# Four token blocks of a mixture layer: transposed indices made ahead, block 3's weights queued behind fixed dots, block 1 alone over 88 value tiles, 48 rows of block 4 in the ring

## The chip, the cores and the metric

One core of a Trainium2 chip runs the whole kernel in one launch. The metric is the device time of an execution in microseconds (us), lower is better. The engines are PE (TensorE), DVE (VectorE), ACT (ScalarE), POOL (GpSimd) and SP (SyncE, which only issues transfers here); each works off its own instructions in order, and 16 DMA engines serve all of them.

## The reference, cut to what matters

The layer is attention, an mLSTM and a merge, and then the channel mixer below, over 512 prompt tokens and 8 sample tokens (D = 1024, 8 heads, top 16, 16384 experts). The change touches only the last part.

```
q   = xb @ wq;  s = q . subkeys            # two halves of 128 keys each
s1, i1 = top_k(s[half 0], 16);  s2, i2 = top_k(s[half 1], 16)
top_s, eidx = the best 16 of s1 + s2;  g = softmax(top_s)
act = gelu(xb . u[eidx])                   # 128 rows of u for each token
out = sum over 128 of (g * act) * v[eidx]  # 128 rows of v for each token
y   = x + out
```

## The kernel before, in words

A scheduler puts the instructions of each engine into a fixed order, by the order in which the source emits them (earlier is more urgent) and by when its own simulation has each one ready. On the chip an engine then waits at each instruction until what it needs is there; nothing overtakes. `tc.issue_after(ins)` puts the instructions of its block that run on the engine of `ins` behind `ins` in that engine's order.

The prompt is four blocks of 128 tokens. Blocks 1 and 2 come from the first half of the prompt (`halves[0]`), blocks 3 and 4 from the second (`halves[1]`).

**u.** For each block `gather` (L1126) issues 128 indirect transfers on POOL (L1115), each with one row of 4 KB for each of 128 tokens (512 KB), into `ring`, a pool of 6 buffers. DVE multiplies each with the block's `xn2` and sums (the dot, L1122) into a column of `S`. `xn2` is one buffer for all blocks, loaded by SP at L1110. After 128 dots `gelu_w` (L1131) makes the final `S` out of them.

**v, blocks 1 to 3.** These multiply weights over all experts with all of v. `w_block` (L1162) makes a block's weights: it transposes `i1`, `i2` and `S` on PE (L1150, copied out of PSUM by ACT at L151), and for each of 32 groups of 4 tokens makes one-hot matrices (DVE at L1173 and L1178, POOL at L1176, ACT at L148 and L1183), multiplies them on PE (L1190) and copies the product into the weights `WT` by ACT (L151). The weights of a block are two halves of 64 tiles, 32 KB a partition each. `v_part` (L1194) then streams v in 128 tiles of 512 KB through 5 buffers (SP, L1196) and, for each block in `use`, does two products of 128x512 (L1200; four instructions). `v_done` adds x and stores.

**v, block 4.** It has no weights: `v_rows_acc` (L1210) gathers 128 rows of v for each token like u (L1214), and DVE adds each, times its `S`, to `acc` (L1216). 

The order at the end, as emitted from L1325 on:

- weights of block 1; `late()` (the top-k of block 4); u of block 3, in which the first step of the sample tokens' top-k is emitted at k = 48
- tiles 0 to 63 for block 1 alone (`JH` = 64)
- weights of block 2, whose PE part stands behind tile 27 (`JW`)
- tiles 64 to 127 for blocks 1 and 2
- u of block 4, with u of the 8 sample tokens between
- weights of block 3, into the buffers of block 1's weights (`wr`, two halves), so not before block 1 is done
- tiles 0 to 63 for blocks 2 and 3, then tiles 64 to 127 for block 3 alone. Beside the latter the rows of block 4: they use `slab`, 16 slots of 4 KB in the two buffers of block 2's weights, and for the first 32 rows every other one uses the ring
- the sample tokens' v rows (L1253, into the ring, multiplied on PE at L1256) and their result (`x1s`, loaded by SP into a buffer of the value tiles)

The lines around the change:

```
useA1 = (v_acc(1), wA1, JH, JH - 1)
for j in range(JH, P):
    v_part(j, [useA0, useA1])
v_done(0, useA0[0])
gather(1, 1, ...)
wB0 = w_new(wr, wr)
w_block(selB[0], wB0, wr, pst_d, 2)
for j in range(JH):
    v_part(j, [useA1] + ([useB0] if j >= JC else []))
```

Of the kernel before, what the change touches and what calls it, by code (L numbers as in the profile page):

```python
# [5 lines left out]
F32 = mybir.dt.float32  # L6
F32R = mybir.dt.float32r
BF16 = mybir.dt.bfloat16
# [7 lines left out]
P = 128  # L16
# [37 lines left out]
EARLY = True  # L54
JH, JC, JW = 64, 0, 27
SLOPES = [2.0 ** (-(h + 1)) for h in range(8)]


def step_kernel(
# [1048 lines left out]
    def gather_dot(d, tok, off, steps, every):  # L1108
        xn2 = keep.tile([P, D], F32, tag="xn2", name="xn2", bufs=1)
        nc.sync.dma_start(xn2, scr_xn2[tok:tok + P])  # L1110
        for k in range(P):
            if steps and k % every == 0:
                next(steps, None)
            gt = ring.tile([P, D], F32, tag="g", name="urow")
            d["rows"] = nc.gpsimd.indirect_dma_start(  # L1115
                out=gt, out_offset=None, in_=u_rows,
                in_offset=bass.IndirectOffsetOnAxis(ap=d["e"][:, k:k + 1], axis=0))
            if off and k % off == off - 1:
                nc.gpsimd.tensor_mul(gt, gt, xn2)
                nc.scalar.activation(gt, gt, AF.Copy, accum_out=d["S"][:, k:k + 1])  # L1120
            else:
                d["dot"] = nc.vector.scalar_tensor_tensor(gt, gt, 1.0, xn2, op0=ALU.mult, op1=ALU.mult,  # L1122
                                                          accum_out=d["S"][:, k:k + 1])

    def gather(hf, i, y=None, steps=None, every=1):
# [19 lines left out]

    def w_prep(sel, pool, pst_):
        out = []
        for key in ("i1", "i2", "S"):
            p = pst_()
            nc.tensor.transpose(p[:, 0:P], sel[key], ident)  # L1150
            t = pool.tile([P, P], BF16 if key == "i1" else F32, tag=f"T_{key}", name=f"T_{key}", bufs=1)
            copy(t, p[:, 0:P])
            out.append(t)
            if key == "i2":
                t = pool.tile([P, P], F32, tag="T_n2", name="T_n2", bufs=1)
                copy(t, p[:, 0:P], scale=-1.0)
                out.append(t)
        return out

    iota4 = []  # L1160

    def w_block(sel, wT, pool, pst_, no):  # L1162
        ONA, PM = ONAS[no], PMS[no]
        if not iota4:
            t = pool.tile([P, P, TG], BF16, name="iota4")
            nc.vector.tensor_copy(t, iota.unsqueeze(2).to_broadcast([P, P, TG]))
            iota4.append(t)
        i1T, i2T, ni2T, sT = w_prep(sel, pool, pst_)
        for g in range(P // TG):
# [10 lines left out]
            for t in range(ONA):  # L1180
                act(b[:, t, :], iota, AF.Abs, bias=ni2T[:, t0 + t:t0 + t + 1])
            if ONA:
# [27 lines left out]
    def v_rows_acc(d, tok, acc, slot):  # L1210
        nc.sync.dma_start(acc, scr_x1[tok:tok + P])
        for k in range(P):
            gt = slot()
            nc.gpsimd.indirect_dma_start(out=gt, out_offset=None, in_=v_rows,  # L1214
                                         in_offset=bass.IndirectOffsetOnAxis(ap=d["e"][:, k:k + 1], axis=0))
            nc.vector.scalar_tensor_tensor(acc, gt, d["S"][:, k:k + 1], acc, op0=ALU.mult, op1=ALU.add)  # L1216
            yield
        nc.gpsimd.dma_start(y_prompt[0, tok:tok + P], acc)

    def sample_peer(py):  # L1220
# [30 lines left out]
        for b in range(NS):  # L1251
# [6 lines left out]
            yield  # L1258
        x1s = dv[0].tile([NS, D], F32, tag="v", name="x1s", bufs=VB)
        nc.sync.dma_start(x1s, scr_x1s)  # L1260
        for q in range(2):
# [5 lines left out]
    for hf in range(2):  # L1267
# [50 lines left out]
        if hf == 1:  # L1318
            alt = [0]

            def pst_w():
                alt[0] ^= 1
                return pst("ao"[alt[0]])

            wA0 = w_new(wr, wr)  # L1325
            w_block(halves[0][0][0], wA0, wr, pst_w, 0)
            late()
            py = []
            steps = sample_peer(py)
            gather(1, 0, None, (next(steps) if k == 48 else None for k in range(P)), 1)  # L1330
            useA0 = ([pst("a"), pst("o")], wA0, 0, P - 1)
            with tc.issue_after(sel[1]["score"].ins):
                mms = [v_part(j, [useA0]) for j in range(JH)]
        if hf == 0 and SV == 1:
# [24 lines left out]

    useA1 = (v_acc(1), wA1, JH, JH - 1)  # L1360
    for j in range(JH, P):
        v_part(j, [useA0, useA1])
    v_done(0, useA0[0])
    gather(1, 1, lambda: wr.tile([P, P], F32, name="ge_y", bufs=1),
           (next(steps) if k % 8 == 4 and k < 68 else None for k in range(P)))
    wB0 = w_new(wr, wr)
    w_block(selB[0], wB0, wr, pst_d, 2)
    useB0 = (v_acc(2), wB0, JC, (JC - 1) % P)
    for j in range(JH):
        v_part(j, [useA1] + ([useB0] if j >= JC else []))  # L1370
# [4 lines left out]
    def gslot():  # L1375
        k = slot_i[0]
        slot_i[0] += 1
        if k < 32:
            return ring.tile([P, D], F32, tag="g", name="vrow") if k % 2 else slab[0][:, k // 2 % 7 + 1, :]
        i = k % 15 + 1  # L1380
        return slab[i // 8][:, i % 8, :]

    run = v_rows_acc(selB[1], HALF + P, slab[0][:, 0, :], gslot)
    for j in [*range(JH, P), *range(JC)]:
        v_part(j, [useB0])
# [44 lines left out]
```

## Time and profile before

| | us |
|---|---|
| median of 3 runs | 2266.93 (2264.25 to 2271.74) |
| the profiled execution's own time | 2271.8 |
| its span (first to last instruction) | 2270.1 |

The profile is of one execution. Times in its rows count from the start of its span. A timeline row gives the start, the time taken, the engine, the line, the operation with its tiles (out<-in), how many were merged, and in brackets how long the engine sat idle before and what ended that. In the rows `ps_a` and `ps_o` are block 1's sums, `y` those of blocks 2 and 3, `ps_w` the products of `w_block` and of the sample rows, `urow` a gathered row of u, `vrow` and `vslab` gathered rows of v, `T_S`, `T_i` the transposed `S`, `i1` and `i2`.

### The profile page before, as it was taken

To read this page: it belongs to the slowest core of one execution; us is meant where nothing else is said; L and a number is where in the kernel's file an instruction comes from. 1 tells how busy PE (TensorE), PEld (TensorE's weight loads), DVE (VectorE), ACT (ScalarE), POOL (GpSimd) and SP (SyncE) were. 2 spreads that over 40 slices of the span, in tenths; PEclk is the share of its full clock that TensorE was granted. 3 is DMA by queue.
4 is the path that set the end of the run, shared out by engine and by line. 5 is a ranking of instruction groups with operands and counts; after the bars stand their busy time and mean duration, and the time that the engine had idled before them with its cause. 6 is when DMAs were issued, how large, how long until landed. Compare 5 with 4: busy or idle time off the path is not lost. (4 is left out here: it accounts for less than half of the span.)

```text
span 2270.1 us, 25459 instructions
## 1 busy us (share of the span) xinstructions
PE 1977.4 (87%) x7694; PEld 1312.6 (58%) x7694; DVE 1536.7 (68%) x3504; ACT 655.4 (29%) x1775; POOL 1307.7 (58%) x1226
## 2 busy tenths in 40 slices
PE   6999999888989999899897984989999699986817
PEld 4675777777878777787775732634445544431202
DVE  2355576787698977777886698855626856536694
ACT  3343233311344433334534315910014600000000
POOL 0487783453486645676776377554415854545573
PEclk9997999999988999999997997999999699997959
DMA  5685776889698889999988297899969899999999
GB/s 158 199 271 203 236 242 214 276 281 325 221 323 286 299 280 340 343 355 340 325 313 321 87 347 262 309 380 409 409 238 355 279 404 409 409 376 417 417 392 369
DMA packets 297803, 704.78 MB, mean 310 GB/s; under 512 B 31518, under 2 KB 157530, under 8 KB 297666
## 3 DMA queue, kind: packets, MB, share of 16 engines
q0 software_dynamic: 114224, 415.84, 49.1%
q1 hardware_dynamic: 183010, 285.74, 35.8%
q10 hardware_dynamic: 432, 1.57, 0.2%
q8 instruction: 61, 1.00, 0.2%
q14 instruction: 76, 0.62, 0.1%
HBM read 684.87 MB, written 18.18 MB: 310 GB/s over the span
## 5 line engine op out<-in xcount | busy, mean ns | idle before, releaser
L1115 POOL DMA_INDIRECT urow<-in_peer_u,k_e x512 | 602.2, 1176 | 394.9 <-DVE urow L1122 279.5
L1122 DVE SCALAR_TENSOR_TENSOR urow<-urow,xn 128x1024 f32<-128x1024 f32 x512 | 643.7, 1267 | 176.4 <-DMA urow<-in_peer_u,k_e 171.7
L1200 PE MATMUL y<-vtile,WT 128*128 128x512 f32 x1024 | 467.4, 601 | 73.6 <-DMA vtile<-in_peer_v 73.1
L291 PE MATMUL ps_mm<-x,wch 128*128 128x264 f32 (+1 forms) x1536 | 384.0, 403 | 27.5 <-DVE sig L315 20.2
L1200 PEld LDWEIGHTS y<-vtile,WT 128*128 128x128 f32 x1024 | 192.2, 192 | 337.5 <-issue 230.2
L291 PEld LDWEIGHTS ps_mm<-x,wch 128*128 128x128 f32 x1536 | 300.4, 200 | 83.9 <-DVE sig L315 23.5
L835 POOL TENSOR_TENSOR kpage<-kpage,qb 128x1024 f32<-128x1024 f32 x64 | 150.2, 2360 | 72.1 <-DMA qb<-scr_q 64.7
L291 PE MATMUL ps_mm<-hT,wch 128*128 128x256 f32 (+1 forms) x768 | 184.8, 390 | 3.9 <-DVE sig L315 3.6
L1214 POOL DMA_INDIRECT vslab<-in_peer_v,k_e x112 | 131.6, 1175 | 87.2 <-DMA vslab<-in_peer_v,k_e 37.7
L1216 DVE SCALAR_TENSOR_TENSOR vslab<-vslab,k_S 128x1024 f32<-128x1024 f32 x112 | 143.9, 1285 | 44.6 <-DMA vslab<-in_peer_v,k_e 41.9
L291 PEld LDWEIGHTS ps_mm<-hT,wch 128*128 128x128 f32 x768 | 143.1, 193 | 26.4 <-DVE sig L315 4.0
L1200 PE MATMUL ps_a<-vtile,WT 128*128 128x512 f32 x256 | 135.4, 611 | 18.4 <-DMA vtile<-in_peer_v 18.3
L296 PE MATMUL ps_mm<-wch,x 128*128 128x256 f32 (+1 forms) x640 | 150.0, 386 | 0.0
L823 POOL DMA_INDIRECT vpage<-in_cache_v,kidx x64 | 79.1, 1236 | 107.6 <-DVE vacc L901 68.1
L1200 PE MATMUL ps_o<-vtile,WT 128*128 128x512 f32 x256 | 132.3, 599 | 0.0
L296 PEld LDWEIGHTS ps_mm<-wch,x 128*128 128x128 f32 (+1 forms) x640 | 108.0, 174 | 29.5 <-issue 2.8
L901 DVE SCALAR_TENSOR_TENSOR vacc<-vpage,aS,vacc 128x128 f32<-128x128 f32 x384 | 110.6, 359 | 18.6 <-DMA vpage<-in_cache_v,kidx 18.4
L148 ACT ACTIVATE oh<-iota,T_n 128x128 f32<-128x128 f32 x352 | 113.4, 403 | 0.1
L1190 PE MATMUL ps_w<-oh,oh 128*128 128x128 f32 x512 | 81.1, 313 | 31.6 <-POOL oh L1176 23.9
L1190 PEld LDWEIGHTS ps_w<-oh,oh 128*128 128x128 f32 x512 | 74.3, 219 | 52.1 <-POOL oh L1176 33.6
L1176 POOL TENSOR_TENSOR oh<-ohe,T_S 128x128 f32<-128x128 bf16 (+1 forms) x96 | 69.7, 733 | 53.2 <-ACT T_S L151 37.3
L836 DVE TENSOR_REDUCE sK<-kpage 128x16 f32<-128x1024 f32 x64 | 77.3, 1211 | 29.1 <-POOL kpage L835 29.0
(428 smaller groups left out, 2728.1 us busy)
## 6 DMA issues: line engine op xcount, KB each, us to landing
vtile<-in_peer_v SPq DMA_DIRECT2D x256, 512.0 KB
wch<-in_w_in SPq DMA_DIRECT2D x256, 256.0 KB
wch<-in_peer_wq SPq DMA_DIRECT2D x64, 256.0 KB
wch<-in_w_branch_a SPq DMA_DIRECT2D x32, 256.0 KB
wch<-in_w_branch_b SPq DMA_DIRECT2D x32, 256.0 KB
wch<-in_w_out SPq DMA_DIRECT2D x32, 256.0 KB
urow<-in_peer_u,k_e POOLq DMA_INDIRECT x512, 7.9
qb<-scr_q SPq DMA_DIRECT2D x8, 512.0 KB
```

Source lines behind the costliest of these rows:

```text
L148: nc.scalar.activation(out, in_, func, bias=b[:n, 0:1] if b.shape[0] != n else b, scale=scale, **kw)
L291: nc.tensor.matmul(out, w[:, c0:c0 + m], xk[:, :n], start=(k == 0 and i == 0), stop=(k == KT - 1 and i == len(tt) - 1))
L296: nc.tensor.matmul(out, x[:, k, t0:t0 + m], ch[k // KP][:, k % KP, :n], start=(k == 0), stop=(k == KT - 1))
L823: nc.gpsimd.indirect_dma_start(out=t, out_offset=None, in_=rows, in_offset=bass.IndirectOffsetOnAxis(ap=kidx[:, b * 8 + pg:b * 8 + pg + 1] ...
L835: (nc.vector if KDV and pg % KDV == KDV - 1 else nc.gpsimd).tensor_mul(kt, kt, qb)
L901: nc.vector.scalar_tensor_tensor(acc[:, h, :], vt[:, h, :], wa, acc[:, h, :], op0=ALU.mult, op1=ALU.add)
L1115: d["rows"] = nc.gpsimd.indirect_dma_start(out=gt, out_offset=None, in_=u_rows, in_offset=bass.IndirectOffsetOnAxis(ap=d["e"][:, k:k + 1], ...
L1122: d["dot"] = nc.vector.scalar_tensor_tensor(gt, gt, 1.0, xn2, op0=ALU.mult, op1=ALU.mult, accum_out=d["S"][:, k:k + 1])
L1190: nc.tensor.matmul(pw[:, t, :], b[:, t, :], a[:, t, :], start=True, stop=True)
L1200: mm = nc.tensor.matmul(py[q], w, vt[:, q * 512:(q + 1) * 512], start=(j == j0), stop=(j == j1))
L1214: nc.gpsimd.indirect_dma_start(out=gt, out_offset=None, in_=v_rows, in_offset=bass.IndirectOffsetOnAxis(ap=d["e"][:, k:k + 1], axis=0))
L1216: nc.vector.scalar_tensor_tensor(acc, gt, d["S"][:, k:k + 1], acc, op0=ALU.mult, op1=ALU.add)
```

## The change

- `w_prep` keeps its transposes with the block, makes only those asked for, in two buffers instead of one, and no longer makes the negated copy `T_n2` (ACT negates the other operand instead). Block 2's three are emitted right behind block 1's weights, ahead of `late()`; block 3's `i1` and `i2` behind block 1's `v_done`; block 3's `S` inside its `w_block`.
- Block 3's `w_block` stands behind block 4's dot 24 on DVE and its gather 30 on POOL.
- Block 1 goes alone over tiles 0 to 87 (`NA` = 88), blocks 1 and 2 over 88 to 127, blocks 2 and 3 over 0 to 87, block 3 alone over 88 to 127.
- The first 48 rows of block 4 all use the ring; `acc` lies in the buffer of `xn2` and is loaded from POOL's queue; `x1s` lies in the ring and is loaded from POOL's queue.

```diff
-JH, JC, JW = 64, 0, 27
+JH, JC, JW, NA, HB = 64, 0, 27, 88, (24, 30)
@@ gather_dot
+            d.setdefault("gets", []).append(d["rows"])
...
+                d.setdefault("dots", []).append(d["dot"])
@@ w_prep
-    def w_prep(sel, pool, pst_):
-        out = []
-        for key in ("i1", "i2", "S"):
+    def w_prep(sel, pool, pst_, keys=("i1", "i2", "S")):
+        T = sel.setdefault("T", {})
+        for key in keys:
             p = pst_()
             nc.tensor.transpose(p[:, 0:P], sel[key], ident)
...
+            T[key] = pool.tile([P, P], BF16 if key == "i1" else F32, tag=f"T_{key}", name=f"T_{key}", bufs=2)
+            copy(T[key], p[:, 0:P])
@@ w_block
-        i1T, i2T, ni2T, sT = w_prep(sel, pool, pst_)
+        w_prep(sel, pool, pst_, [k for k in ("i1", "i2", "S") if k not in sel.get("T", {})])
+        i1T, i2T, sT = (sel["T"][k] for k in ("i1", "i2", "S"))
...
-                act(b[:, t, :], iota, AF.Abs, bias=ni2T[:, t0 + t:t0 + t + 1])
+                act(b[:, t, :], iota, AF.Abs, scale=-1.0, bias=i2T[:, t0 + t:t0 + t + 1])
@@ v_rows_acc
-        nc.sync.dma_start(acc, scr_x1[tok:tok + P])
+        nc.gpsimd.dma_start(acc, scr_x1[tok:tok + P])
@@ sample_peer
-        x1s = dv[0].tile([NS, D], F32, tag="v", name="x1s", bufs=VB)
-        nc.sync.dma_start(x1s, scr_x1s)
+        x1s = ring.tile([NS, D], F32, tag="g", name="x1s")
+        nc.gpsimd.dma_start(x1s, scr_x1s)
@@ the order
             w_block(halves[0][0][0], wA0, wr, pst_w, 0)
+            w_prep(halves[0][0][1], wr, pst_w)
             late()
...
-                mms = [v_part(j, [useA0]) for j in range(JH)]
+                mms = [v_part(j, [useA0]) for j in range(NA)]
...
-    useA1 = (v_acc(1), wA1, JH, JH - 1)
-    for j in range(JH, P):
+    useA1 = (v_acc(1), wA1, NA, NA - 1)
+    for j in range(NA, P):
         v_part(j, [useA0, useA1])
     v_done(0, useA0[0])
+    w_prep(selB[0], wr, pst_d, ("i1", "i2"))
...
-    w_block(selB[0], wB0, wr, pst_d, 2)
+    with tc.issue_after(selB[1]["dots"][HB[0]].ins), tc.issue_after(selB[1]["gets"][HB[1]].ins):
+        w_block(selB[0], wB0, wr, pst_d, 2)
...
-    for j in range(JH):
+    for j in range(NA):
         v_part(j, [useA1] + ([useB0] if j >= JC else []))
...
-        if k < 32:
-            return ring.tile([P, D], F32, tag="g", name="vrow") if k % 2 else slab[0][:, k // 2 % 7 + 1, :]
+        if k < 48:
+            return ring.tile([P, D], F32, tag="g", name="vrow")
...
-    run = v_rows_acc(selB[1], HALF + P, slab[0][:, 0, :], gslot)
-    for j in [*range(JH, P), *range(JC)]:
+    acc = keep.tile([P, D], F32, tag="xn2", name="acc", bufs=1)
+    run = v_rows_acc(selB[1], HALF + P, acc, gslot)
+    for j in [*range(NA, P), *range(JC)]:
         v_part(j, [useB0])
```

## Rows read from the trace of the kernel before

**Rows 1.** Windows by stage: us, five engines' busy time, clock, DMA share, GB/s

```profile
1305.00:1505.00 200.00, 152.29 (x532) 78.33 (x532) 163.16 (x495) 100.79 (x292) 134.62 (x170) 0.93 0.85 314
1505.00:1731.00 226.00, 221.02 (x525) 98.58 (x524) 114.37 (x193) 6.56 (x19) 92.33 (x93) 0.99 0.93 364
1731.00:1811.00 80.00, 54.19 (x264) 43.50 (x262) 70.47 (x127) 65.68 (x196) 62.28 (x67) 0.75 0.83 291
1811.00:2024.00 213.00, 212.34 (x493) 93.65 (x494) 110.82 (x195) 2.93 (x9) 100.49 (x99) 1.00 1.00 397
2024.00:2270.00 246.00, 143.90 (x288) 48.70 (x286) 164.64 (x131) 0.00 (x0) 140.25 (x123) 0.83 0.99 399
```

**Rows 2.** Windows of the whole end and of single stretches, same columns

```profile
1305.00:2265.00 960.00, 783.22 (x2097) 362.77 (x2096) 622.38 (x1135) 175.96 (x514) 529.98 (x550) 0.92 0.94 365
...
1367.00:1395.00 28.00, 0.40 (x3) 0.14 (x1) 23.25 (x68) 6.92 (x14) 24.66 (x28) 0.59 0.62 218
...
1655.00:1697.00 42.00, 42.00 (x112) 19.66 (x111) 5.52 (x11) 3.69 (x12) 2.74 (x5) 1.00 0.55 204
...
2024.00:2163.00 139.00, 101.65 (x204) 33.27 (x202) 89.07 (x71) 0.00 (x0) 84.46 (x72) 0.90 1.02 415
2163.00:2218.00 55.00, 1.98 (x4) 0.68 (x4) 52.94 (x43) 0.00 (x0) 41.30 (x40) 0.54 1.00 387
```

**Rows 3.** Timeline of PE, block 1 alone and then with block 2

```profile
1338.36 1.12 PE L1200 MATMUL ps_a<-vtile,WT 128*128 128x512 f32 x2 [0.56 <-DMA vtile<-in_peer_v]
...
1340.91 1.13 PE L1200 MATMUL ps_a<-vtile,WT 128*128 128x512 f32 x2 [0.57 <-DMA vtile<-in_peer_v]
...
1395.40 0.47 PE L1150 MATMUL ps_w<-ident,k_S 128*128 128x128 f32 x1 [28.00 <-ACT T_i L151]
...
1519.00 1.88 PE L1200 MATMUL y<-vtile,WT 128*128 128x512 f32 x4
...
1522.43 1.88 PE L1200 MATMUL y<-vtile,WT 128*128 128x512 f32 x4
...
1729.47 1.02 PE L1200 MATMUL ps_o<-vtile,WT 128*128 128x512 f32 x2
```

**Rows 4.** Timeline of DVE: first one-hot of block 2

```profile
1398.95 1.39 DVE L1173 TENSOR_TENSOR ohe<-iota,T_i 128x512 bf16<-128x512 bf16 x3
```

**Rows 5.** Timeline of DVE: block 3's last dot, its first one-hots, block 4's first dot

```profile
1650.20 1.23 DVE L1122 SCALAR_TENSOR_TENSOR urow<-urow,xn 128x1024 f32<-128x1024 f32 x1 [0.87 <-DMA urow<-in_peer_u,k_e]
...
1689.57 1.23 DVE L1178 TENSOR_TENSOR oh<-ohe,T_S 128x384 f32<-128x384 bf16 x2 [34.24 <-ACT T_S L151]
...
1695.46 1.21 DVE L1122 SCALAR_TENSOR_TENSOR urow<-urow,xn 128x1024 f32<-128x1024 f32 x1
```

**Rows 6.** Timeline of SP's queue: block 4's load of xn2

```profile
1679.22 0.42 SPq L1110 DMA_DIRECT2D xn<-scr_xn  x1
```

**Rows 7.** Window of urow's instructions: DVE (two records a dot), POOL, clock, DMA

```profile
1505.00:1655.00 150.00, 88.26 (x144) 67.39 (x70) 0.99 1.03 408
```

**Rows 8.** Groups by line, 1731 to 1811: busy, mean ns, idle before

```profile
L1115 POOL DMA_INDIRECT urow<-in_peer_u,k_e x31 | 37.8, 1219 | 11.0 <-issue 4.9 <-DVE urow L1122 3.9 <-DVE urow_s L1244 1.2
L151 ACT ACTIVATE WT<-ps_w 128x256 f32<-128x256 f32 x61 | 20.0, 382 | 14.3 <-PE ps_w L1190 14.1
L1183 ACT ACTIVATE oh<-oh,one 128x512 f32<-128x512 f32 x27 | 19.1, 727 | 0.1
```

**Rows 9.** Timeline of POOL: sample rows, the wait for block 2, the last store

```profile
1994.75 0.94 POOL L1253 DMA_INDIRECT vrow_s<-in_peer_v,eT  x1 [0.30 <-DVE ge_y L1137]
...
2022.52 0.94 POOL L1214 DMA_INDIRECT vslab<-in_peer_v,k_e  x1 [19.17 <-PE y L1200]
...
2260.18 0.59 POOL L1218 DMA_DIRECT2D out_y_prompt<-vslab  x1 [19.46 <-DVE vslab L1216]
```

**Rows 10.** Timeline of PE: the first product of sample rows

```profile
2023.89 1.88 PE L1256 MATMUL ps_w<-vrow_s,wz 128*8 128x512 f32 x4
```

**Rows 11.** Waits of SP's queue, 1650 to 2270

```profile
SPq L1196 <- DMA out_y_sample<-x1s: 55.8, 1, 55.8
```

More of the change, by code (lines that the diff above doesn't have):

```diff
@@ L1144, in w_new @@
         return [(pool.tile([P, JH, P], F32, tag="WT", name="WT", bufs=2), JH * i) for i, pool in enumerate(pools)]
-    def w_prep(sel, pool, pst_):
-        out = []
-        for key in ("i1", "i2", "S"):
+    def w_prep(sel, pool, pst_, keys=("i1", "i2", "S")):
+        T = sel.setdefault("T", {})
+        for key in keys:
             p = pst_()
             nc.tensor.transpose(p[:, 0:P], sel[key], ident)
[L1151 to L1158, printed above, removed]
+            T[key] = pool.tile([P, P], BF16 if key == "i1" else F32, tag=f"T_{key}", name=f"T_{key}", bufs=2)
+            copy(T[key], p[:, 0:P])
     iota4 = []
```

## The prediction

> **What bounds the kernel now.** The windows by stage come first, since every edit lies behind 1305 us. They show five stages [rows 1]: block 1 alone (200 us), blocks 1 and 2 (226), block 3's weights (80), blocks 2 and 3 (213), block 3 alone beside block 4's rows (246). The reader is to look at the DMA share and at PE together. Stage 4 is PE's (212 of 213 us), stage 2 nearly so. Stage 5 is the DMA's: share 0.99, PE 144 of 246. Stage 3 is neither's: PE 54 of 80, DMA 0.83. Over the whole end DMA moved 365 GB/s on average, where full stretches show 408 and 415 [rows 2, 7], so some 11% of 960 us, about 105 us, is DMA time left unused. Single stretches then say where: 28 us at 218 GB/s and 42 us at 204 [rows 2], beside stage 3 at 291 [rows 1].
>
> Timelines say why. At 1367 PE stands 28 us before block 2's third transpose, waiting for an ACT copy [rows 3], while DVE and POOL work off block 4's top-k (23 and 25 of 28 us) [rows 2]; ACT's copy stands in order behind its own share of that. At 1655 block 3's dots are done, but DVE's next instruction is a one-hot of block 3 that waits 34 us for `T_S`, which PE transposes only where its order has it; block 4's dots are queued behind, and the first runs at 1695.46 [rows 5]. With the ring full, gathers stop: that is the 204 GB/s.
>
> **The rule weighed.** Stretches of 139 and 150 us ran at 415 and 408 GB/s [rows 2, 7], and the sums below go by 415. The Trainium skill ("DMA: Bandwidth & Descriptors", Specifications) gives HBM about 358 GB/s per core; by that figure the end, at 365, would have no DMA time left, and the sum would come to nothing. The trace disagrees with it, by those two stretches.
>
> **The change part by part.** I compare with the profiled execution (span 2270, own time 2271.8, 4.9 us above the median of the runs, 2266.93) and carry the difference to the median.
>
> *1. 24 tiles for block 1 alone (64 to 87).* With block 2 a tile takes 3.43 us (1519.00 to 1522.43), PE's own pace; alone, beside gathers, 2.55 (1338.36 to 1340.91), where PE waits for the tile [rows 3]. So block 1 ends 24 x (3.43 - 2.55) = 21 us sooner. Block 2's 24 products move to stage 4.
>
> *2. Block 2's transposes ahead.* The 28 us [rows 3] can go wholly or stay under another name: DVE, at 23 of 28 us, makes one-hots only behind the top-k, the first at 1398.95 [rows 4], and PE reaches their products at the same place behind tile 27. Ends 0 and -28. Two groups can be ready beforehand (`OH1` = 2), each worth 2.86 us: stage 3 took 80 us for its last 28 groups (L1183 runs once a group, 27 times in the stage, the first groups having come earlier), with ACT busy for 66 of them [rows 1, 8]. I take -6, because DVE's row is the nearest. The transposes and copies themselves, and the three copies less, are under 0.5 us each and lie beside other work; should PE meet them before block 2's `S` is there, the bound is the 28 us of the same kind of wait. So block 1 ends at 1731 - 21 - 6 = 1704 (1682 to 1710).
>
> *3. The gate.* Gathers of block 3 get 2.08 us each beside stage 2 (144 records, two a dot, in 150 us [rows 7]) and 2.55 beside single tiles; 24 tiles at 2.55 are 61 us, 24 gathers instead of 29, so its last dot moves from 1651 to about 1662. DVE and POOL no longer stand in the 34 us wait. With the load of `xn2` (an estimate of 5 us: 0.524 MB at half of 415 GB/s are 2.5 us, doubled for what is queued ahead) block 4's dot 0 runs at 1667 instead of 1695. By 1704 18 of 25 dots are done; 7 more at about 1.6 us (no tiles are being loaded then; POOL's 1.22 and a gap [rows 8] is the lower bound, 2.08 the upper) put the gate at 1715, 11 us behind block 1's end. What is queued behind it: DVE's and POOL's one-hots, and on PE all but five tiles of block 2.
>
> *4. Block 3's weights.* 32 groups, none ahead on DVE; three of ACT's can be (`OHB` = 3). 29 x 2.86 = 83 us (80 to 91): done at 1798, before 1811: -13.
>
> *5. Stage 4.* five tiles, of which block 2's part was done in stage 3, at 1.72 (half of 3.43) and 83 at 3.43: 293 us, to 2091. The same working gives 211 for the 213 before [rows 1]. Gathers here: of u, 128 - 30 - 31 [rows 8] = 67, then 48 rows of v and 8 sample rows, 123 x 2.08 = 256 us, below 293, so all 48 can be in. `acc` loaded from POOL's queue waits for block 4's last dot with the v gathers behind it; about the six buffers of the ring, 6 x 2.08 = 12 us, covered by the 37 left over. Without that cover what is late goes to stage 5 at 1.26 us a row.
>
> *6. Stage 5.* 35 tiles and 80 rows are 115 x 0.524 MB / 415 GB/s = 145 us, and from the last add to the end 10 us, as after 2260.18 [rows 9]: 2246. POOL's wait of 19 us for block 2's buffers [rows 9] goes for the first 48 rows, which need none of them; it is late next at row 48, at the end of stage 4. `x1s` leaves the tiles' buffers: SP waited 56 us for its store [rows 11], but DMA then still ran at 387 GB/s [rows 2], so at most 55 x (1 - 387/415) = 4 us, not counted. SP loses two transfers; POOL gains two of about 0.6 us.
>
> Sum: -13 (weights ready), +80 (stage 4), -91 (stage 5 with its end) = -24; median 2266.9 - 24 = **2243 us**.
>
> **The rivals.**
>
> *A. More.* The gate falls no later than block 1's end, because block 3's gathers run ahead: weights start at 1704, or at 1682 if the 28 us go too. Weights done 11 to 33 us sooner: 2210 to 2232. For it: 24 dots need only 50 us. Against: in the sum they get 37. 0.20.
>
> *B. Slower: the load of `xn2` stands behind tiles in SP's queue.* Before, it was issued at 1679.22 [rows 6], 28 us after the buffer was free (last dot 1650.20 [rows 5]), as SP's order has it behind tile loads that wait for buffers. With block 1 ending sooner, that place can be behind the last of its tiles: block 4's dot 0 at about 1706, 25 dots with sample rows between at 1.6 to 2.08 us, 45 us, gate 1751, weights done 1834, end 36 us later than my sum: 2279. It decides from a dot 0 later than about 1691 (24 us after my 1667). Against it: gathers were 28 us ahead of that order, which is leeway the other way too. 0.20.
>
> *C. No change: the ring fills with sample rows.* A sample row holds a ring buffer until PE multiplies it; the first, issued at 1994.75 [rows 9], was multiplied at 2023.89, after stage 4 [rows 10]. One is emitted for every four rows, so after 24 rows all six buffers could be held until stage 4 ends. Then 24 rows more fall to stage 5: +30 us, 2273. Against: at 1994 stage 4 had only 30 us left. 0.13.
>
> *D. No change: DMA is at its limit already.* If the mean of 365 GB/s [rows 2] were all that DMA sustains over such a mix, the same bytes would take the same time in any order: 2267. Against it: two long stretches at 408 and more [rows 2, 7]. 0.04. This is what the page's figure above would mean.
>
> **How the numbers follow.** My sum has 0.43. Faster by over 0.3% (7 us, about what a measurement of this kernel can tell from no change): the sum and A, 0.63, and a little of B where the 28 us go as well (its 2279 falls to 2257): 0.65. Within 0.3%: C and D less a third, 0.13. Slower: B's rest and C's longer end, 0.22. The sum's own bounds (the gate by 2.08 instead of 1.6, weights 80 to 91, stall 0 to -28, 4 us of `x1s`) reach from 2226 to 2256; the range goes on to A's middle and to B: 2214 to 2281.
>
> **What would show it.** Right: PE's 28 us before L1150 gone, with a shorter wait for DVE's or POOL's one-hots near 1370; no 34 us wait for `T_S`; block 4's dot 0 near 1667; weights of block 3 ready near 1798; stage 4 of some 293 us with PE full and gathers of v in it from about 1945; stage 5 of some 150 us. Wrong: a dot 0 behind 1700 (B); fewer than 30 rows of v gathered before block 2 ends (C); PE idle inside stage 4; a weights stage longer than 91 us, or a stall of PE ahead of 1305, where block 2's transposes now stand.

## The result and the profile after

The changed kernel takes 2294.84 us (median of 7 runs, 2288.67 to 2305.27), the kernel before beside it 2271.74 (7 runs, 2260.3 to 2281.0). The ratio is 1.0119, 95% interval 1.0089 to 1.0150: **slower by about 27 us** by the ratio (23 by the two medians), where 24 us faster was forecast, and above the range (2214 to 2281). The profiled execution is the longest of its seven (own time 2305.27, span 2303.6), so its stages, not its total, are what to compare.

The first view is the windows by stage of the changed kernel (window, length, busy time of PE, PE's weight loads, DVE, ACT and POOL with records, PE's clock, DMA share, GB/s). The boundaries: start of the double tiles, end of block 1, first products of block 3's weights, their end, end of block 2.

```profile
1310.00:1575.00 265.00, 200.00 (x615) 96.21 (x615) 193.26 (x536) 93.86 (x272) 159.68 (x195) 0.91 0.90 336
1575.00:1713.00 138.00, 137.43 (x322) 60.66 (x321) 68.93 (x117) 1.88 (x5) 53.34 (x56) 1.00 0.98 387
1713.00:1752.00 39.00, 12.58 (x25) 4.65 (x24) 28.03 (x49) 0.00 (x0) 25.28 (x24) 0.71 0.94 343
1752.00:1848.00 96.00, 60.96 (x263) 52.55 (x264) 90.28 (x162) 71.65 (x212) 83.66 (x84) 0.62 0.84 284
1848.00:2154.00 306.00, 305.34 (x706) 129.34 (x705) 140.37 (x185) 1.91 (x5) 126.05 (x123) 1.00 0.93 358
2154.00:2304.00 150.00, 80.47 (x165) 27.91 (x163) 99.66 (x80) 0.00 (x0) 82.30 (x70) 0.85 0.96 388
```

Beside [rows 1] the reader sees five stages become six: there is a new one of 39 us in which PE works 12.6. Since both kernels move the same bytes (length times rate, summed, is 351 MB in each), the DMA rate is a ledger of what each stage costs. Against 400 GB/s, about the rate of the last two stages before, a stage loses its length times (1 - rate/400):

| stage | lost before, us | lost after, us |
|---|---|---|
| block 1, alone and with block 2 | 43 + 20 | 42 + 4 |
| gate and block 3's weights | 22 | 6 + 28 |
| blocks 2 and 3 (stage 4) | 2 | 32 |
| the last stage | 1 | 4 |

That is 88 us before, 116 after: 17 us are won ahead of block 1's end, 12 are lost at the gate and the weights, 30 in stage 4. The ledger is accounting: it says in which stage time is lost, not why.

The second view is the timeline of DVE from block 3's last dot to the gate.

```profile
1667.04 1.23 DVE L1123 SCALAR_TENSOR_TENSOR urow<-urow,xn 128x1024 f32<-128x1024 f32 x1 [0.51 <-DMA urow<-in_peer_u,k_e]
...
1685.22 1.23 DVE L1123 SCALAR_TENSOR_TENSOR urow<-urow,xn 128x1024 f32<-128x1024 f32 x1 [13.06 <-DMA xn<-scr_xn]
...
1712.07 0.69 DVE L1204 TENSOR_TENSOR x1r<-x1r,ps_a 128x512 f32<-128x512 f32 x1 [6.38 <-PE ps_a L1197]
...
1736.85 1.23 DVE L1241 SCALAR_TENSOR_TENSOR urow_s<-urow_s,xb 128x1024 f32<-128x1024 f32 x1 [3.38 <-DMA xb<-scr_xn2s]
...
1745.44 1.14 DVE L1170 TENSOR_TENSOR ohe<-iota,T_i 128x512 bf16<-128x512 bf16 x3
```

The 34 us before `T_S` [rows 5] are gone, and block 4's dot 0 is 10 us earlier. But DVE then stands in order: 13 us for `xn2`, 6 for block 1's last product (its addition comes after only nine dots), and the first one-hot of block 3, which ran at 1689 before, runs at 1745. On PE the two waits are:

```profile
1404.70 2.08 PE L1187 MATMUL ps_w<-oh,oh 128*128 128x128 f32 x8 [30.45 <-POOL oh L1173]
...
1751.78 0.58 PE L1187 MATMUL ps_w<-oh,oh 128*128 128x128 f32 x1 [22.24 <-POOL oh L1173]
```

The first answers to the 28.00 us of [rows 3]: the wait has another name and the same length. The second is new. In block 3's weights the groups by line (1752 to 1846; busy and mean ns, then idle before) show two engines nearly full:

```profile
L1123 DVE SCALAR_TENSOR_TENSOR urow<-urow,xn 128x1024 f32<-128x1024 f32 x43 | 53.9, 1261 | 2.1 <-DMA urow<-in_peer_u,k_e 1.9
L1115 POOL DMA_INDIRECT urow<-in_peer_u,k_e x44 | 52.5, 1194 | 10.5 <-issue 6.8 <-DVE urow L1123 1.8 <-DVE urow_s L1241 0.9
```

43 dots and 44 gathers stand among the one-hots, where 31 gathers did [rows 8]: 13 gathers more at 1.19 us are 15 us more of POOL's time, and the stage is 16 us longer. DVE, with their dots, is busy 90 of 96 us. That the extra gathers and dots make the length is read from these rows and not tested by itself; the last section shows a second difference in them, POOL's one-hots lasting longer beside dots. In stage 4, windows of 20 us around its end (2154) and the timeline of POOL show the DMA going idle:

```profile
2100.00:2120.00 20.00, 20.00 (x48) 8.90 (x47) 13.92 (x11) 0.00 (x0) 6.48 (x5) 1.00 0.84 331
2120.00:2140.00 20.00, 20.00 (x48) 8.86 (x47) 1.49 (x2) 0.00 (x0) 2.97 (x3) 1.00 0.69 252
2140.00:2160.00 20.00, 20.00 (x48) 8.81 (x47) 1.37 (x2) 0.00 (x0) 4.30 (x5) 1.00 0.58 198
2160.00:2180.00 20.00, 14.96 (x31) 4.93 (x29) 10.11 (x8) 0.00 (x0) 10.34 (x11) 1.00 1.03 420
```

```profile
2154.48 0.94 POOL L1211 DMA_INDIRECT vslab<-in_peer_v,k_e  x1 [30.90 <-PE y L1197]
```

By 2124 the 48 rows are gathered, and eleven more into the first of block 2's two buffers; for the second POOL waits 31 us, where it waited 19 [rows 9]. Some 20 of the 32 us lost in stage 4 are lost here. Most of the rest is lost from 1970 to 2072, at 321 to 376 GB/s, where POOL waits 36 us in all for products of sample rows, which hold buffers of the ring, and 18 for DVE's additions. The sample products run in this stage, eight of this form (timeline of PE):

```profile
2007.88 1.88 PE L1253 MATMUL ps_w<-vrow_s,wz 128*8 128x512 f32 x4
```

### The profile page after: what moved, and what is told of

Read it like the earlier page. It is cut to its first block, busy times and chain, and to the rows that moved or that the text cites. A ratio compares the mean times of both kernels' runs of the same rounds, so it can differ in the third digit from the quotient of the medians.

```text
span 2303.6 us, 25448 instructions
## 1 busy us (share of the span) xinstructions
PE 1991.1 (86%) x7694; PEld 1321.9 (57%) x7694; DVE 1537.8 (67%) x3504; ACT 653.3 (28%) x1772; POOL 1308.9 (57%) x1228
## 5 line engine op out<-in xcount | busy, mean ns | idle before, releaser
L1197 PE MATMUL y<-vtile,WT 128*128 128x512 f32 x1024 | 460.8, 599 | 26.2 <-DMA vtile<-in_peer_v 25.8
L1187 PE MATMUL ps_w<-oh,oh 128*128 128x128 f32 x512 | 92.6, 343 | 89.8 <-POOL oh L1173 82.3
L1211 POOL DMA_INDIRECT vslab<-in_peer_v,k_e x80 | 93.6, 1170 | 96.3 <-DMA vslab<-in_peer_v,k_e 32.2
L1187 PEld LDWEIGHTS ps_w<-oh,oh 128*128 128x128 f32 x512 | 84.1, 247 | 109.0 <-POOL oh L1173 97.0
L1213 DVE SCALAR_TENSOR_TENSOR acc<-vslab,k_S,acc 128x1024 f32<-128x1024 f32 x80 | 102.8, 1286 | 44.8 <-DMA vslab<-in_peer_v,k_e 43.0
L148 ACT ACTIVATE oh<-iota,T_i 128x128 f32<-128x128 f32 x352 | 114.0, 406 | 0.1
L1213 DVE SCALAR_TENSOR_TENSOR acc<-vrow,k_S,acc 128x1024 f32<-128x1024 f32 x48 | 61.6, 1284 | 69.5 <-DMA vrow<-in_peer_v,k_e 61.9
L1197 PEld LDWEIGHTS ps_a<-vtile,WT 128*128 128x128 f32 x256 | 44.9, 196 | 98.7 <-DMA vtile<-in_peer_v 68.6
```

What stands on the lines that cost most here:

```text
L148: nc.scalar.activation(out, in_, func, bias=b[:n, 0:1] if b.shape[0] != n else b, scale=scale, **kw)
L1187: nc.tensor.matmul(pw[:, t, :], b[:, t, :], a[:, t, :], start=True, stop=True)
L1197: mm = nc.tensor.matmul(py[q], w, vt[:, q * 512:(q + 1) * 512], start=(j == j0), stop=(j == j1))
```

## The experiments

Block 1's first product lies between 1290 and 1313 us in these profiles, with the work upstream the same, so stages are counted from that product. Ratios are against the kernel before, run on the same chip.

| run | ratio, 95% interval | first product to end, us |
|---|---|---|
| kernel before | 1 | 964 |
| the change | 1.0119 (1.0089 to 1.0150) | 993 |
| e1 no gate | 1.0094 (1.0060 to 1.0128) | 984 |
| e2 64 tiles | 1.0084 (1.0055 to 1.0114) | 981 |
| e3 ring undone | 1.0256 (1.0221 to 1.0291) | 1019 |
| e4 `xn2` from ACT | 1.0116 (1.0086 to 1.0145) | 995 |
| f1 96 rows in the ring | 1.0113 (1.0087 to 1.0138) | 993 |
| f2 sample rows last | 1.0132 (1.0104 to 1.0160) | 991 |
| f3 f1, f2 and no gate | 1.0133 (1.0103 to 1.0163) | 991 |
| f4 `JW` = 44 | 1.0022 (0.9995 to 1.0049) | 967 |
| i1 gate sooner | 1.0064 (1.0036 to 1.0092) | 977 |
| i2 `JW` = 44, no gate | 0.9986 (0.9959 to 1.0013) | 961 |
| g1 64 tiles, no gate | 1.0081 (1.0052 to 1.0110) | 979 |
| g2 the same, `JW` = 36 | 0.9997 (0.9970 to 1.0024) | 958 |
| before and 88 tiles (g3) | 1.0005 (0.9978 to 1.0033) | 968 |
| before and ring (h1) | 1.0038 (1.0009 to 1.0067) | 978 |
| before and transposes (h2) | 1.0033 (1.0000 to 1.0066) | 973 |
| before and gate (h4) | 1.0114 (1.0075 to 1.0153) | 994 |
| before and `JW` = 36 (g0) | 0.9964 (0.9934 to 0.9993) | 955 |
| before, 88 tiles, `JW` = 44 (h3) | 0.9901 (0.9866 to 0.9935) | 947 |

### One thing taken from the change

**e1: no gate.**

```
-    with tc.issue_after(selB[1]["dots"][HB[0]].ins), tc.issue_after(selB[1]["gets"][HB[1]].ins):
-        w_block(selB[0], wB0, wr, pst_d, 2)
+    w_block(selB[0], wB0, wr, pst_d, 2)
```

> The changed kernel without the gate: block 3's weights wait for nothing but their operands, the rest of the change stays. Theory (the gate costs the time): block 3's first one-hot runs within 5 us of block 1's end near 1712 instead of at 1745, its weights are done near 1815 instead of 1846, and the time falls by 20 to 30 us, to a ratio of 0.998 to 1.003 against the kernel before. Rival (the gate only moves dots from behind the weights to ahead of them, and the same gathers have to be made later): weights done earlier as well, but block 4's dots end later and its rows of v move to the last stage, so the time falls by less than 10 us, ratio 1.008 to 1.013.

Measured: the weights' last product ends 489 us behind the first product, against 534, and the time falls by only 0.25%, with intervals that overlap. The windows of stage 4 and the last stage say where 45 us went:

```profile
1782.00:2085.60 303.60, 303.60 (x701) 130.88 (x700) 143.06 (x224) 2.81 (x8) 133.39 (x131) 0.99 0.96 376
2085.60:2275.80 190.20, 85.71 (x176) 30.02 (x174) 136.54 (x109) 0.00 (x0) 103.35 (x97) 0.77 0.96 378
```

The last stage is 40 us longer: gathers of u that the gate had ahead of the weights now lie in stage 4, and rows of v fall to the end. The rival is right: a sooner start of the weights is paid back in gathers.

**e2: 64 tiles** (`NA` 88 to 64).

> The changed kernel with 64 tiles for block 1 alone instead of 88. Theory (PE stands idle ahead of the gate, so what the 24 tiles save ahead of it is lost, and their products come back in stage 4 at 1.7 us each): block 1 ends near 1731, the gate falls at about the same 1745, stage 4 has 24 double tiles fewer, and the time falls by 10 to 25 us, ratio 1.001 to 1.008. Rival (the 24 tiles save their 21 us as step 1 of the prediction has it, and the loss is elsewhere): the gate and everything behind it come 15 to 20 us later, ratio 1.018 to 1.022.

The gate falls 453 us behind the first product against 435, the weights end 18 us later, stage 4 is 226 us at 395 GB/s, the last stage 203 instead of 150. The time is 8 us lower, short of what was expected, with overlapping intervals: the 24 tiles are no gain and nearly no loss.

**e3: ring undone** (the fourth part put back as it was: `slab[0][:, 0, :]` as sum, 32 rows alternating, both loads on SP).

> The changed kernel with the old buffers for block 4's rows of v, its sum and the sample rows' sum (the fourth part of the change undone). Theory (rows of v in the ring help, though the sample rows hold buffers of it): in stage 4 only some 10 rows are gathered before POOL waits for block 2's weights, 110 and more are left for the last stage, which grows by 25 to 45 us: ratio 1.022 to 1.032. Rival (the ring is full of sample rows anyway, so that part neither helps nor hurts): within 7 us of the changed kernel, ratio 1.009 to 1.015.

31 us slower than the change, as the theory had it: stage 4 falls to 331 GB/s, the last stage is 174 us. In the kernel with the gate and 88 tiles, rows of v in the ring are worth 1.4%.

**e4: `xn2` for block 4 from ACT's queue.**

```
-        nc.sync.dma_start(xn2, scr_xn2[tok:tok + P])
+        (nc.scalar if tok == HALF + P else nc.sync).dma_start(xn2, scr_xn2[tok:tok + P])
```

> The changed kernel with block 4's load of xn2 issued from ACT's queue instead of SP's, where it stands behind tile loads; nothing else moves. Theory (rival B of the prediction: that place in the queue makes the gate late): block 4's dot 0 runs near 1674 instead of 1685, the gate near 1735 instead of 1745, and the time falls by 8 to 12 us, ratio 1.006 to 1.009. Rival (the gate is set by how fast gathers come and by what else DVE has in its order, not by dot 0): dot 0 near 1674 too, but the gate within 4 us of 1745 and the time within 5 us, ratio 1.010 to 1.013.

DVE's timeline shows the dot where it was expected, and what is late next:

```profile
1675.76 1.22 DVE L1123 SCALAR_TENSOR_TENSOR urow<-urow,xn 128x1024 f32<-128x1024 f32 x1 [4.80 <-DMA xn<-scr_xn]
...
1712.71 0.69 DVE L1204 TENSOR_TENSOR x1r<-x1r,ps_a 128x512 f32<-128x512 f32 x1 [17.27 <-PE ps_a L1197]
...
1744.99 1.09 DVE L1170 TENSOR_TENSOR ohe<-iota,T_i 128x512 bf16<-128x512 bf16 x3
```

Dot 0 is 9.5 us sooner (7 counted from block 1's first product), nine dots run, and DVE then stands 17.27 us instead of 6.38 before block 1's addition. The gate is at 1745 as before. The rival's numbers came. Block 4's load of `xn2` is late, and sparing that alone gains nothing.

### Stage 4 given more to fetch

**f1:** `if k < 96` instead of 48. **f2:** the sample rows taken out of the loop of tiles:

```
             next(run, None)
-            if j % 4 == 3:
-                next(steps, None)
```

**f3:** both, without the gate.

> The changed kernel with the first 96 rows of block 4 in the ring instead of 48. The changed kernel's stage 4 (308 us, blocks 2 and 3 together) runs at 358 GB/s where the kernel before had 399, and POOL stands 31 us there before a slab that block 2's weights still hold. Theory (stage 4 is long because PE is full, and has too few gathers that may run in it): that wait goes, some 14 rows more are added before block 2 ends (55 to 60 instead of 43), and the time falls by 12 to 20 us, ratio 1.003 to 1.007. Rival (the six buffers of the ring, held by the sample rows, are the limit and not the number 48): no more than 5 rows more, time within 5 us of the changed kernel, ratio 1.010 to 1.014.

> The changed kernel with the sample rows' gathers of v and their products emitted behind block 4's rows instead of one behind every fourth tile. Theory (sample rows hold ring buffers in stage 4, and their products lengthen it): the eight products of 1.9 us leave stage 4, which falls from 308 to about 293 us, POOL no longer waits for them, more rows are added before block 2 ends, and the time falls by 10 to 20 us, ratio 1.003 to 1.008. Rival (they only move into the last stage, where each costs the 1.3 us of its gather): stage 4 shorter by 15 us and the last stage longer by as much, time within 5 us, ratio 1.010 to 1.014.

> The two edits just named and the gate taken away as well, the rest of the change stays. Theory (each fills DMA time of its own: 5 us of the gate, some 15 of the 96 rows, some 10 of the sample rows): weights of block 3 done about 490 us behind block 1's first product, stage 4 at 390 GB/s or more, time 25 to 35 us below the changed kernel, ratio 0.995 to 1.002. Rival (they fill the same gap): the gain is that of the largest one alone, ratio 1.002 to 1.008.

None gives anything. f1 does what it was to do in stage 4 (63 rows added in it instead of 52, by DVE's records; the 43 in its expectation is too low) and loses it at once, as its windows of the two last stages and DVE's waits from 2151 on show:

```profile
1851.00:2159.00 308.00, 308.00 (x712) 130.81 (x713) 156.44 (x200) 2.06 (x6) 140.97 (x141) 1.00 0.99 384
2159.00:2306.70 147.70, 80.40 (x166) 28.04 (x164) 85.61 (x69) 0.00 (x0) 53.01 (x54) 0.86 0.87 342
```

```profile
DVE acc L1213 <- DMA vrow<-in_peer_v,k_e: 57.2, 30, 21.2
```

```profile
2258.28 42.23 DVE L1213 SCALAR_TENSOR_TENSOR acc<-vslab,k_S,acc 128x1024 f32<-128x1024 f32 x32
```

POOL's order gathers slab rows ahead of ring rows that DVE adds first. DVE stands 57 us for these, the slab rows lie landed behind, and the last 32 additions run alone at 1.32 us. In f2 the sample rows no longer hold buffers, the 48 rows are used up sooner and DMA runs at 212 and 132 GB/s in the two windows ahead of 2140, while the products still run in stage 4 (305 us). In f3, where they do leave it, stage 4 is 295 us at 384 GB/s and the last stage 206 at 355. Theory and numbers fell in all three: stage 4's lost 32 us of DMA are not a loss that can be taken away by itself.

### The place of block 2's weights

**f4:** in the changed kernel `JW` 27 to 44. **g0:** in the kernel before `JW` 27 to 36.

> The changed kernel with block 2's weights behind tile 44 instead of tile 27 (JW). Theory (PE's 30 us ahead of block 2's first products, during which DMA runs at some 200 GB/s, are the place in PE's order and not the late operands): PE goes on with tiles 28 to 43 there, the wait falls below 8 us, block 1 ends 10 to 20 us sooner counted from its first product, and the time falls by 5 to 12 us, ratio 1.006 to 1.010. Rival (block 1 ends sooner but the gate waits for the same gathers of block 4): the gain ahead of the gate is lost in it, time within 4 us, ratio 1.010 to 1.014.

> The kernel before with one number changed: block 2's weights behind tile 36 instead of tile 27. Theory (the 28 us in which PE waits for an ACT copy are a place in PE's order): PE goes on with tiles 28 to 36 there, the wait falls below 10 us, DMA no longer falls to 218 GB/s in it, block 1 ends 10 to 20 us sooner counted from its first product, and the time falls by 8 to 20 us, ratio 0.991 to 0.997. Rival (block 2's weights then end later than tile 64 is reached, and PE waits there instead): time within 6 us, ratio 0.997 to 1.003.

f4 gains more than was expected, g0 what was expected, and the reason given was half wrong. The wait was to fall below 8 and 10 us. In g0 it is 25 us in two pieces (6.56 and 18.89), and in f4 it does not go at all:

```profile
1438.24 2.08 PE L1187 MATMUL ps_w<-oh,oh 128*128 128x128 f32 x8 [28.25 <-POOL oh L1173]
```

What changes is what runs beside it. These are the windows of the wait, first of the changed kernel, then of f4:

```profile
1370.00:1390.00 20.00, 4.24 (x22) 2.70 (x20) 19.01 (x69) 4.38 (x11) 16.02 (x24) 0.69 0.72 265
1390.00:1410.00 20.00, 5.30 (x20) 3.79 (x21) 14.60 (x24) 9.48 (x26) 16.01 (x17) 0.54 0.52 167
```

```profile
1409.00:1429.00 20.00, 0.99 (x3) 0.17 (x1) 14.90 (x26) 1.49 (x3) 15.97 (x14) 0.65 0.95 336
1429.00:1449.00 20.00, 9.86 (x41) 6.83 (x42) 17.31 (x32) 7.43 (x24) 10.25 (x12) 0.66 0.85 321
```

At tile 27 DVE is full of block 4's top-k (69 records in 20 us); some six dots run in a window, five and seven gathers are issued, and in the second window no tile is loaded either. At tile 44 the top-k is over and dots take DVE's time, 13 in the first window with 14 gathers, which carry DMA while PE stands. The stage up to the double tiles rises from 336 to about 368 GB/s and block 1 ends 20 us sooner. All of it lasts to the end: f4 is 22 us below the change.

### The parts alone, and combinations

**g3, h1, h2, h4** put one part each on the kernel before: `NA` = 88 for `JH` in the five lines that count tiles; the ring's part; the transposes; the gate around `w_block` of block 3. **g1** is the change without gate and with 64 tiles (transposes and ring are left).

> The kernel before with 88 tiles for block 1 alone instead of 64, and nothing else of the change. Theory (what is saved ahead is lost in stage 4, where PE is full for 24 double tiles more while there are no gathers left that may run): block 1 ends some 20 us sooner, stage 4 lasts 295 to 310 us with DMA below 360 GB/s in it, and the time is 15 to 45 us above the kernel before, ratio 1.006 to 1.020. Rival (step 1 of the prediction: 21 us saved, and DMA catches up in the last stage): ratio 0.989 to 0.997.

> The changed kernel with 64 tiles and without the gate, so that of the change only the transposes ahead and the ring's part are left. Theory (88 tiles and the gate together are the loss): stage 4 near 225 us at 395 GB/s, no idle stretch of PE between block 1's end and block 3's weights, time back at that of the kernel before, ratio 0.995 to 1.003. Rival (taken away one by one they gave 6 and 8 us, and no more than that is theirs): ratio 1.004 to 1.009.

> The kernel before with the fourth part of the change alone (first 48 rows of v in the ring, sum in the buffer of xn2, both small loads on POOL's queue). Theory (where stage 4 has gathers of u enough, no row of v starts in it, and in the last stage the 48 rows go through six buffers that sample rows share, where before they had some fourteen): last stage 8 to 12 us longer at 386 to 390 GB/s, ratio 1.002 to 1.007. Rival (the 18 us that are left without the 88 tiles and the gate belong to the transposes): ratio 0.996 to 1.001.

> The kernel before with the transposes ahead alone (block 2's, and two of block 3's). Theory (block 2's weights end some 8 us sooner, but tile 64, where they are first wanted, comes no sooner): ratio 0.996 to 1.002. Rival (the transposes and copies stand in the way of something in PE's or ACT's order): ratio 1.003 to 1.010.

> The kernel before with the gate alone (25 dots and 31 gathers of block 4 ahead of block 3's weights). Theory (the gate spends gathers of u ahead of stage 4, and without rows of v in the ring stage 4 then runs out of gathers): PE idle some 20 us ahead of the gate, stage 4 below 380 GB/s, ratio 1.008 to 1.025. Rival (the gate costs its own wait alone, or nothing where the dots come in time): ratio 0.998 to 1.006.

g3 came out between theory and rival. Its last two stages:

```profile
1797.00:2106.00 309.00, 308.76 (x712) 130.74 (x712) 158.63 (x234) 2.81 (x8) 140.40 (x137) 1.00 0.98 384
2106.00:2276.60 170.60, 80.77 (x166) 28.02 (x164) 120.42 (x97) 0.00 (x0) 97.99 (x86) 0.81 0.96 388
```

Block 1 ends 20 us sooner and the weights 17, and stage 4 with the last one takes 480 us where it took 459 [rows 1]: the gain comes back as DMA time lost there, 12 and 5 us by the ledger, where it was 2 and 1.

h4 is the part that costs. Its windows of the gate, the weights, stage 4 and the last stage:

```profile
1720.00:1747.00 27.00, 11.71 (x27) 4.67 (x25) 21.03 (x37) 0.00 (x0) 16.77 (x16) 0.82 0.95 344
1747.00:1840.00 93.00, 59.26 (x256) 52.12 (x256) 86.85 (x157) 71.95 (x211) 81.10 (x83) 0.61 0.85 288
1840.00:2071.00 231.00, 227.39 (x520) 94.40 (x521) 122.38 (x172) 2.45 (x8) 114.65 (x107) 0.99 0.98 387
2071.00:2289.00 218.00, 125.48 (x261) 47.50 (x259) 120.23 (x97) 0.00 (x0) 99.69 (x86) 0.84 0.92 361
```

27 us of gate, weights of 93 us instead of 80, stage 4 at 387 GB/s, the last at 361. By the ledger that is 4 + 26, 8 and 21 us, where the kernel before has 22, 2 and 1: the theory's ratio came, but its stage 4 below 380 GB/s did not, and most of the loss lies in the last stage. There SP's waits and PE's timeline show another cause than gathers used up:

```profile
SPq L1198 <- DMA out_y_sample<-x1s: 74.6, 1, 74.6
```

```profile
2241.06 43.71 PE L1202 MATMUL y<-vtile,WT 128*128 128x512 f32 x96 [68.16 <-DMA vtile<-in_peer_v]
```

The sample rows' result still lies in a buffer of the value tiles, so SP's tile loads stand 75 us behind its store, where they stood 56 before [rows 11]. Block 4's rows are all added at 2234, and 24 tiles are then left to run without them, at 258 GB/s. In the change `x1s` lies in the ring, and its last stage runs at 388 GB/s; this fits e1, where taking the gate away gained 0.25% and not 1.1%. It is read from rows alone: no run has the gate with `x1s` moved and nothing else.

h1 shows the other side of e3: without a gate no row of v starts in stage 4, the 48 rows go through six buffers in the last stage, and it is 257 us at 385 GB/s (POOL waits 22 us there for sample products). h2's +0.33% reaches zero with its interval; its profile has 4 us more in the weights and no wait that says why. Its cause is open, and the change without its transposes was not tried. g1's 1.0081 is about what h1 and h2 give together (1.0071).

So the four parts alone sum to +1.9%, and together measure +1.2%: the ring's part, a loss alone, pays where the gate has used up the gathers of u. No single part is the loss: without the gate, the ring and the transposes cost about as much (g1) as the whole change does.

### Is it the gate's lateness?

**i1:** e4's edit, and block 1's two additions on DVE behind dot 24:

```
-    v_done(0, useA0[0])
...
+    with tc.issue_after(selB[1]["dots"][HB[0]].ins):
+        v_done(0, useA0[0])
```

> The changed kernel with xn2 of block 4 from ACT's queue as above, and block 1's two last additions on DVE put behind dot 24 of block 4 instead of behind dot 8, where DVE stood 17 us for PE. Theory (the late gate is not what costs; early dots use up the gathers that stage 4 needs): the gate falls 10 to 20 us sooner, some 415 to 427 us behind block 1's first product instead of 437, but stage 4 has fewer gathers left, its DMA rate falls below 358 GB/s, and the time stays within 8 us of the changed kernel, ratio 1.007 to 1.014. Rival (step 3 of the prediction: everything behind the gate moves with it): time 12 to 20 us below, ratio 1.001 to 1.006.

The rival is nearer. The gate is 21 us behind block 1's end instead of 33, and the windows of weights, stage 4 and last stage simply follow:

```profile
1735.00:1825.00 90.00, 61.69 (x262) 52.88 (x263) 84.97 (x155) 72.07 (x211) 77.43 (x82) 0.62 0.87 300
1825.00:2132.00 307.00, 307.00 (x711) 130.30 (x711) 143.81 (x193) 2.25 (x7) 136.72 (x126) 1.00 0.94 362
2132.00:2281.70 149.70, 80.76 (x166) 28.00 (x164) 99.89 (x80) 0.00 (x0) 83.07 (x70) 0.85 0.96 389
```

Stage 4 and the last stage keep their length, 307 and 150 us. The time is 12 us below the change (1.0064 against 1.0119, intervals that just overlap at 1.009). Lateness of the gate is thus nearly half of the loss, as far as these intervals tell. My theory, that sooner dots would starve stage 4, fell: its rate rose to 362.

### Versions

**g2** is g1 with `JW` = 36, **h3** is g3 with `JW` = 44, **i2** the change with `JW` = 44 and no gate (h3 with ring and transposes).

> The changed kernel with 64 tiles, without the gate, and with block 2's weights behind tile 36. Theory (the same wait taken away here): 8 to 20 us below the run with 64 tiles and no gate, ratio 0.988 to 0.996, faster than the kernel before. Rival (the wait comes back ahead of tile 64): the same as that run within 5 us.

> The kernel before with 88 tiles for block 1 alone and block 2's weights behind tile 44. Theory (the wait of 28 us goes, as it did in the changed kernel with the same number, which fell by 22 us): block 1 ends some 40 us sooner than in the kernel before counted from its first product, ratio 0.987 to 0.994, the fastest of the runs. Rival (stage 4, full of PE, and the last stage give it back, as they did with the 88 tiles alone): ratio 0.996 to 1.002.

> The changed kernel with block 2's weights behind tile 44 and without the gate; it differs from the fastest run so far (0.990) by the transposes ahead and the ring's part alone. Theory (these two, 1.003 and 1.004 alone, cost about as much here): ratio 0.994 to 1.000. Rival (with 88 tiles stage 4 is long enough for rows of v, and the ring's part pays for itself there): ratio 0.987 to 0.993.

h3 beats both kernels, by 1.0% the kernel before (2251.16 us, median of 8 runs). Its windows up to block 1's end and of stage 4:

```profile
1302.40:1568.00 265.60, 212.89 (x661) 103.12 (x660) 203.67 (x563) 101.55 (x292) 176.92 (x205) 0.94 0.95 366
1568.00:1687.50 119.50, 119.50 (x292) 53.91 (x291) 65.62 (x114) 6.11 (x17) 53.01 (x54) 1.00 0.96 376
1687.50:1770.00 82.50, 56.03 (x265) 43.83 (x263) 71.94 (x129) 65.74 (x195) 65.21 (x66) 0.74 0.83 284
1770.00:2079.50 309.50, 308.90 (x712) 131.13 (x713) 159.02 (x234) 3.48 (x10) 144.75 (x139) 1.00 0.98 386
```

Block 1 ends 384 us behind its first product, against 424 before and 401 in the change; stage 4 and the last stage are those of g3. Of these 40 us some 17 are left at the end (947 us against 964): the 20 of the 88 tiles are paid back as in g3, the other 20 are nearly kept. The theory's ratio came, but not its reason: PE's wait ahead of block 2's products is 30.68 us in h3, so here too it was moved and not taken away. g2 is 19 us below g1, at the upper end of what was expected, but only level with the kernel before, since g1 was slower than its own theory had it. i2 gives what the ring and the transposes cost beside h3, 0.9986 against 0.9901: with 88 tiles and no gate they don't pay either.

## Why the prediction was wrong

The sum's marks against the profile: block 1's end 1704, seen 1712 (+8, of which 5 lie ahead of block 1's first product, at 1310.41 instead of 1305.59); gate 11 us behind it, seen 33 (+22); from the gate to the weights' end 83 us, seen 101 (+18); stage 4 293, seen 308 (+15); last stage and end 155, seen 150 (-5). Together +58, from 2246 to 2304.

- **Step 1 (24 tiles, -21): right where it looked.** g3 has block 1's end 20 us sooner. What the step left out is that this gain is paid back in stage 4 and after: 1.0005 in all.
- **Step 2 (the stall, -6, ends 0 and -28): the end 0.** The wait has POOL's one-hot as its name instead of an ACT copy and is 30 us. Block 2's weights do end some 9 us sooner, but with 64 tiles (e2) block 1 ends no sooner for it. The row to read was not the wait but the windows beside it: f4 and g0 gain by moving it, not by shortening it.
- **Step 3 (gate at 1715) failed first.** It counted gathers and their pace, and not DVE's order. Between dots 8 and 9 of block 4 stands block 1's addition, which waits for PE's last product, so no more than nine dots can run ahead of block 1's end however soon dot 0 is; three sample dots stand among the rest, one of which waits 3.4 us for its `xb`. The prediction had 18 of the 25 dots done by block 1's end; nine were. It asked what is queued behind the gate, and not what is queued among the instructions that the gate waits for. i1, which takes away the addition and the late `xn2`, prices it: 12 us.
- **Step 4 (83 us) was mis-sized:** 93 us in its products alone. It took a group's pace from a stage with 31 gathers; behind the gate the order puts 44 gathers and 43 dots among 32 groups, and DVE is full; PE waits 28 us there for POOL's one-hots, where it waited 18 before. h4, with a gate, has 93 us too, h3 without one 82.
- **Step 5 (293 us) left out a term** that the prediction had in hand: eight sample products of 1.88 us [rows 10], put into a stage that PE fills, are the 15 us; f3, where they leave it, has 295. The count of gathers came out near by luck: 67 of u, 48 rows and 8 sample rows, 123, against 53 (the other 13 and one more had run ahead of it), 59 and 8, 120, in the trace.
- **Step 6 was right** to 5 us (the 31 us at row 48 are what it said would be late next).
- **Rivals.** A's condition failed, with the gate 33 us behind block 1's end. B had the sign, and its load was late (1680.57 as against 1679.22 before), but dot 0 ran at 1685, ahead of the 1691 from which B was to decide, and e4 shows that the load alone costs nothing. C's ring does fill (POOL waits 36 us in all for sample products in stage 4), but 52 rows and not 24 were added before block 2's end, and f2 shows no gain from freeing it. D is refuted by h3, which moves the same bytes at 370 GB/s.

The deeper fault is that the sum was a chain of marks. The DMA ledger of the first section would have asked, of every us won ahead, whether the later stages lose it again; in e1, f1, f3 and g3 they did. In f4 and i1 they did not: there stage 4 and the last stage kept their length.

## What to carry to other kernels

Where an edit waits for the n-th of a row of instructions, list what else stands among those n on their engine, and what each of those waits for. Where several stages share one total of bytes, keep a ledger of bytes and rate per stage: a stage that ends sooner gains only what the later ones do not lose again. And a stall that cannot be taken away can be moved to where other engines have work that fills the shared resource, which here gave 22 us for one number.

## What the runs showed of the hardware

A dot of 128x1024 mostly takes 1.20 to 1.23 us, but 1.97 to 2.70 in six places beside block 4's top-k on POOL. These are DVE's dots beside the top-k in the changed kernel, and POOL's arithmetic that overlaps the slow one:

```profile
1375.90 2.54 DVE L1123 SCALAR_TENSOR_TENSOR urow<-urow,xn 128x1024 f32<-128x1024 f32 x1
...
1383.22 1.20 DVE L1123 SCALAR_TENSOR_TENSOR urow<-urow,xn 128x1024 f32<-128x1024 f32 x1
```

```profile
1376.10 1.25 POOL L1017 TENSOR_TENSOR tk_eq<-tk_eq,tk_sf 128x512 f32<-128x512 f32 x1
1377.43 1.15 POOL L1004 TENSOR_SCALAR tk_p<-tk_pf 128x16 f32<-128x16 f32 x1
...
1382.90 1.03 POOL L1115 DMA_INDIRECT urow<-in_peer_u,k_e  x1 [1.37 <-DVE tk_sv L980]
```

Beside a gather's issue the dot keeps its 1.20 us; beside POOL's operations of 128x512 it can double. It is not always the dot that is long. In block 3's weights a one-hot of POOL can be, where a dot runs beside it:

```profile
1796.67 1.21 DVE L1123 SCALAR_TENSOR_TENSOR urow<-urow,xn 128x1024 f32<-128x1024 f32 x1
```

```profile
1796.68 1.46 POOL L1173 TENSOR_TENSOR oh<-ohe,T_S 128x128 f32<-128x128 bf16 x1
...
1806.15 0.45 POOL L1173 TENSOR_TENSOR oh<-ohe,T_S 128x128 f32<-128x128 bf16 x1
```

The second one-hot has no dot beside it. These one-hots take 776 ns on average in the change's weights stage, with 43 dots, and 639 in that of the kernel before, with 33; how much of the stage's 16 us that is was not tested. The Trainium skill ("GPSIMD Engine Reference", 1. Specifications) says that POOL shares its SBUF interfaces with VectorE and names instructions with two SBUF inputs, as the dot has; these rows agree, though no run here took POOL's operations or the dots away.

PE's granted clock in block 3's weights was 0.61 (h4) and 0.62 (the change), where PE had been busy 12 of 27 and 13 of 39 us just before, and 0.74 (h3) and 0.75 [rows 1], where it had been busy 119.5 of 119.5 and 221 of 226 us: means between its two levels, 1.2 and 2.4 GHz. A product there took 405 ns in the change against 349 in h3. PE was busy for 61 of the 96 us, and 28 of the 35 us that it waited were for POOL's one-hots, so its clock was hardly the bound.
